# Three quarters of the second feed-forward product as Strassen's seven products, in place of eight

## The chip, the cores and the metric

The kernel runs on one core of one Trainium2 chip. The metric is the device time of one execution in microseconds; the median of the timed runs is compared. TensorE (PE) multiplies, VectorE (DVE) and ScalarE (ACT) work element by element, GpSimd (POOL) does a little arithmetic, and the DMA queues of SyncE (SP) and ACT bring the weights in. In the profile "PEld" is the loading of the stationary operand into TensorE.

## The reference, cut to what matters

Two blocks run one after the other over 512 tokens of 1024 features. The first has two layers, each a mixture of a dilated attention and an mLSTM and then a feed-forward part; the second has two mixers (an MLA and a gated linear attention), each steered by scale, shift and gate rows that come from a condition vector (`modulation`). The change is in the feed-forward part of the first block:

```python
D_MODEL = 1024
SEQ = 512
D_FF = 4 * D_MODEL
...
    h2 = rms_norm(x, norm_mlp_w)
    x = x + jnp.square(jax.nn.relu(h2 @ w_ff1)) @ w_ff2
    return x
```

All of it is float32. `w_ff1` is 1024 x 4096 and `w_ff2` is 4096 x 1024 in each of the two layers.

## The kernel before, in words

**Exact products.** Every large product is made of three matmuls in the type float32r: each operand is split into a high and a low part (`Prog.split`: ACT writes the high part, L246, and DVE subtracts it from the source, L247), and `mm3` (L274 to L277) multiplies high by high, high by low and low by high into one PSUM bank. A matmul holds a 128 x 128 stationary tile and streams 512 columns (256 in one place).

**The feed-forward part** (`first_block`, L666 to L704) goes in steps b of 512 of the 4096 hidden features. A *feature step* takes one unit of `w_ff1` (128 x 1024 numbers, loaded by the SP queue into `raw`, split into `spl`), issues 24 matmuls into a bank of the pool A, and evacuates it: ACT takes the relu (L678), DVE squares it (L679), and ACT and DVE split the square into the two parts of `big`. In the first step of a layer each of the four units is used in two half steps of 256 tokens. Four feature steps give 512 hidden features of all 512 tokens. `add_wide` (L732) then multiplies them with four units of `w_ff2`: eight groups of 12 matmuls, each evacuated by DVE into the residual stream `x` (L737). The last 512 features are added token tile by token tile, so that the next stage's norm can begin.

**Beside it: the modulation rows** (`Modulation`, L787 to L827). `start` loads the conditions (`cond`, on the ACT queue), takes a tanh on ACT (L803) and a product on DVE (L804) and issues the first two loads of `ada` on the ACT queue. Each of 24 calls of `use` per layer then reduces one 128 x 1024 unit of `ada` with three DVE instructions (L817 twice, L819 once) and issues a load two units ahead (L810). Its tiles come from the pools that the whole first block shares, so its instructions may be placed as soon as the attention's tiles are free.

**What sets the order.** A scheduler turns the program into one list of instructions for each engine, and each engine works its list strictly from the front. An instruction that must wait holds up everything behind it on its engine; a DMA issue on the ACT list is such an instruction too. Tiles come from pools with a fixed number of places; a new tile waits until the last reader of the old one in its place is done. In the feed-forward part the pool A has two banks, `spl` four places and `raw` two.

## Time and profile before

| quantity | value |
|---|---|
| median of 3 runs (lowest to highest) | 2380.8 us (2378.7 to 2384.31) |
| span of the profiled execution | 2376.0 us |
| PE busy | 2336.0 us, 98% of the span, 12280 matmuls |
| DVE busy | 1438.8 us, 61% |
| ACT busy | 961.2 us, 40% |
| POOL busy | 48.5 us, 2% |
| chain that ended last | PE 84%, DVE 8%, ACT 3%, DMA 2%, issue 2% |

The profiled execution's own time is its span; the median of the timed runs is 4.8 us above it, and all working below is made against the span. Matmuls are pipelined, so the busy time of one (377 ns in the mean for the largest group) is not the distance from one to the next; that distance is read from a stretch that PE fills. The page's granted clock of TensorE reads 9 (full speed) in each of its 40 slices.

### The profile page before, as it was taken

Reading aid. Unit: us, or ns where it says so; the run is one execution under the profiler, and the core shown is the slowest. Engines: PE = TensorE matmul, PEld = TensorE weight load, DVE = VectorE, ACT = ScalarE, POOL = GpSimd, SP = SyncE. Lnnn points to the kernel's source line nnn. Section 1 sums busy time; section 2 is a strip of 40 time slices with the busy share of each in tenths; the row PEclk is TensorE's granted clock in tenths of the full one; section 3 lists DMA queues with packets and bytes.
Section 4 is the critical chain, followed back from the end, with each engine's and each line's share of the span. In section 5 each row is a group of like instructions: output and inputs, shape, how many; then the busy total and the mean of one; then the engine's idle time right before and its main releaser. Section 6 shows DMA issues by size and latency. Waiting matters only on the chain.

```text
span 2376.0 us, 30969 instructions
## 1 busy us (share of the span) xinstructions
PE 2336.0 (98%) x12280; PEld 1904.2 (80%) x12280; DVE 1438.8 (61%) x2534; ACT 961.2 (40%) x1809; POOL 48.5 (2%) x96
## 2 busy tenths in 40 slices
PE   8999999999999999999999999999999999999998
PEld 6777888888888777788888888789888888788886
DVE  4477795544444547779654444454477776647486
ACT  3356422422322226642342232333366783363332
POOL 0000000000000000000000000010000000000000
PEclk9999999999999999999999999999999999999999
DMA  4221463222323222146432222312110130121111
GB/s 152 80 82 48 166 215 124 92 94 89 106 89 99 83 80 72 54 152 215 136 106 98 89 98 98 97 39 89 45 28 19 24 88 22 59 88 36 48 51 71
DMA packets 61345, 209.24 MB, mean 88 GB/s; under 512 B 8576, under 2 KB 9872, under 8 KB 60944
## 3 DMA queue, kind: packets, MB, share of 16 engines
q1 hardware_dynamic: 54000, 179.99, 23.4%
q10 hardware_dynamic: 7200, 27.27, 3.5%
q8 instruction: 97, 1.59, 0.3%
q14 instruction: 48, 0.39, 0.1%
HBM read 201.99 MB, written 2.10 MB: 86 GB/s over the span
## 4 chain that ended last, share of the span: by engine, by line
PE 84%; DVE 8%; ACT 3%; DMA 2%; issue 2%; POOL 1%; SPq 0%; ACTq 0%; POOLq 0%; DVEq 0%
PE A L277 22%; PE A L276 22%; PE A L275 21%; PE O L1133 2%; PE T L1125 2%; DVE spl L247 2%; PE S L275 1%; PE O L512 1%; PE S L276 1%; PE S L277 1%; PE S L486 1%; DMA ada<-in_ada 1%; PE T L506 1%; DVE junk L817 1%; ACT spl L246 1%
## 5 line engine op out<-in xcount | busy, mean ns | idle before, releaser
L246 ACT ACTIVATE spl<-raw 128x1024 fp32r<-128x1024 f32 (+2 forms) x313 | 325.0, 1040 | 477.0 <-PE A L277 429.6
L275 PE MATMUL A<-big,spl 128*128 128x512 f32 (+1 forms) x1280 | 483.0, 377 | 1.9 <-DVE x L737 1.2
L277 PE MATMUL A<-big,spl 128*128 128x512 f32 (+1 forms) x1280 | 481.4, 376 | 0.2 <-DVE spl L247 0.2
L276 PE MATMUL A<-big,spl 128*128 128x512 f32 (+1 forms) x1280 | 480.8, 376 | 0.0
L247 DVE TENSOR_TENSOR spl<-raw,spl 128x1024 fp32r<-128x1024 f32 (+2 forms) x313 | 375.8, 1204 | 163.1 <-ACT spl L246 161.7
L276 PE MATMUL A<-spl,big 128*128 128x512 f32 (+2 forms) x992 | 384.7, 389 | 1.1 <-DVE spl L247 1.0
L275 PE MATMUL A<-spl,big 128*128 128x512 f32 (+2 forms) x992 | 383.6, 388 | 1.6 <-ACT big L246 0.8
L277 PE MATMUL A<-spl,big 128*128 128x512 f32 (+2 forms) x992 | 381.8, 385 | 0.2 <-DVE ms L284 0.2
L277 PEld LDWEIGHTS A<-big,spl 128*128 128x128 f32 x1280 | 241.1, 188 | 45.9 <-issue 2.6
L275 PEld LDWEIGHTS A<-big,spl 128*128 128x128 f32 x1280 | 241.2, 188 | 45.1 <-DVE x L737 1.6
L276 PEld LDWEIGHTS A<-big,spl 128*128 128x128 f32 x1280 | 241.2, 188 | 43.3 <-issue 1.4
L275 PEld LDWEIGHTS A<-spl,big 128*128 128x128 f32 x992 | 186.3, 188 | 44.2 <-ACT big L246 2.8
L276 PEld LDWEIGHTS A<-spl,big 128*128 128x128 f32 x992 | 186.7, 188 | 40.3 <-DVE spl L247 3.0
L277 PEld LDWEIGHTS A<-spl,big 128*128 128x128 f32 x992 | 186.6, 188 | 39.2 <-issue 1.5
L737 DVE SCALAR_TENSOR_TENSOR x<-A,x 128x512 f32<-128x512 f32 x160 | 110.0, 688 | 121.7 <-PE A L277 119.9
L679 DVE TENSOR_TENSOR r<-r 128x512 f32<-128x512 f32 (+1 forms) x72 | 45.5, 633 | 170.9 <-ACT r L678 170.9
L678 ACT ACTIVATE r<-A 128x512 f32<-128x512 f32 (+1 forms) x72 | 39.7, 551 | 219.8 <-PE A L277 219.6
L1100 DVE TENSOR_REDUCE mx<-S 128x1 f32<-128x768 f32 (+1 forms) x80 | 71.8, 900 | 26.7 <-PE S L277 25.8
L1126 ACT ACTIVATE pt<-T 128x512 f32<-128x512 f32 (+1 forms) x144 | 66.5, 501 | 32.2 <-PE T L1125 31.1
L286 POOL TENSOR_TENSOR rstd<-ms,mhalf 128x1 f32<-128x1 f32 (+2 forms) x68 | 42.4, 623 | 1765.1 <-DVE ms L284 1720.8
L1105 ACT ACTIVATE p<-S,mx 128x768 f32<-128x768 f32 (+1 forms) x96 | 72.6, 760 | 13.8 <-DVE mx L1100 12.9
L817 DVE SCALAR_TENSOR_TENSOR junk<-ada,cond 128x512 f32<-128x512 f32 x96 | 65.7, 687 | 6.1 <-DMA ada<-in_ada 4.9
(413 smaller groups left out, 3438.8 us busy)
## 6 DMA issues: line engine op xcount, KB each, us to landing
raw<-in_wl SPq DMA_DIRECT2D x244, 512.0 KB, 3.2
ada<-in_ada ACTq DMA_DIRECT2D x48, 512.0 KB, 3.8
raw<-in_gla SPq DMA_DIRECT2D x33, 512.0 KB, 3.2
raw<-in_mla SPq DMA_DIRECT2D x20, 512.0 KB, 3.3
raw<-in_mla SPq DMA_DIRECT2D x8, 384.0 KB, 2.9
qT<-rot SPq DMA_DIRECT2D x32, 96.0 KB, 2.8
x<-in_x SPq DMA_DIRECT2D x4, 512.0 KB, 10.2
big<-in_wl SPq DMA_DIRECT2D x4, 512.0 KB, 9.3
```

Of the source, the lines that this page charges most:

```text
L246: nc.scalar.activation(hi, src, AF.Copy)
L247: nc.vector.tensor_tensor(lo, src, f32(hi), op=OP.subtract)
L275: mm(ps, lh, rh, start=start, stop=False)
L276: mm(ps, lh, rl, start=False, stop=False)
L277: mm(ps, ll, rh, start=False, stop=stop)
L737: P.nc.vector.scalar_tensor_tensor(xv, ps, scale, xv, op0=OP.mult, op1=OP.add)
L817: nc.vector.scalar_tensor_tensor(junk, w[:, o], 0.5, self.cond[:, 0, o], op0=OP.mult, op1=OP.mult, accum_out=self.acc[:, g, j:j + 1])
L1100: nc.vector.tensor_reduce(mx[:, 0:two], pss[:, 0:two * m].rearrange("p (t n) -> p t n", t=two), AX.X, OP.max, negate=True)
L1105: nc.scalar.activation(p[:, t * m:(t + 1) * m], pss[:, t * m:(t + 1) * m], AF.Exp, bias=mx[:, t:t + 1], accum_out=sl[:, t:t + 1])
L1125: nc.tensor.transpose(pst[:, k:k + 128], p[:, o + k:o + k + 128], P.ident)
L1126: nc.scalar.activation(pt[:, o:o + w], pst[:, 0:w], AF.Copy)
L1133: nc.tensor.matmul(weigh.o[64 * i:64 * i + 64, (t0 + t) * 128:(t0 + t + 1) * 128], V[4 * c + k][:, h * 64:(h + 1) * 64], pts[i][:, t * m + ...
```

## The change

The first 3072 of the 4096 hidden features are taken in three chunks of 1024. For a chunk the second product is a 2 x 2 block product: token halves (256) by feature halves (512) times feature halves by column halves (512). The class `Seven` computes it with seven block products (24 matmuls each) of sums of quarters, in place of eight; the remaining 1024 features go through `add_wide` as before. A chunk's seven products stand in turn with the eight feature steps of the next chunk.

- The squares stay whole (float32) in `big` or `hidden`; sums of their quarters (`total`, on DVE, L867) or the quarters themselves are split for each product (`part`).
- The quarters of `w_ff2` are loaded as tiles of 128 x 2048 (`quarter`); sums of them are made in place on POOL (`gather`, L863, two halves of 128 x 1024 each), and two units are split for each product. There are four gathers, eight POOL instructions, in a chunk.
- The products accumulate in two pairs of banks, X and Y, that stay allocated; after a product DVE adds the bank, with a sign, into `x` (L850), and a later product goes on accumulating on what stands there.
- The pools of the attention and the mLSTM are closed before the feed-forward part, and its own pools are opened in their place. `mod.start` takes its tiles from these new pools, and `use` takes its `junk` from the pool `relu`, of two places, which also holds the relu's output.
- Comments and blank lines differ throughout (left out here), and the DMA scratch is set to 1024.

```diff
+QUARTERS = ((0, 0), (0, 1), (1, 1), (1, 0))
...
     f1, f2 = a["w_ff1"][l], a["w_ff2"][l]
-    for b in range(9):
-        if b < 8:
-            u += [_tall(f1, 512 * b + 128 * j) for j in range(4)]
-        if b:
-            for ch in range(2):
-                u += [_wide(f2, 4 * (b - 1) + k, 512 * ch) for k in (0, 2)]
+    u += [_tall(f1, 128 * j) for j in range(32)]
+    for b in (6, 7):
+        for ch in range(2):
+            u += [_wide(f2, 4 * b + k, 512 * ch) for k in (0, 2)]
     return np.stack(u)
+
+def pack_quarters(a, l):
+    w = a["w_ff2"][l][0:3072].reshape(3, 2, 4, 128, 2, 512).transpose(0, 1, 4, 3, 2, 5)
+    return np.stack([w[:, i, j] for i, j in QUARTERS], axis=1).reshape(12, 128, 2048)
...
     for l in range(2):
+        mixing = ExitStack()
+        rest = P.pool("big", 1, mixing, side="right")
+        vp, tmp, one, pp = (P.pool(n, k, mixing) for n, k in (("vp", 1), ("tmp", 2), ("one", 1), ("pp", 3)))
...
+        mixing.close()
         act2 = act_of(norm.dst)
+        after = ExitStack()
+        vp, tmp, one = (P.pool(n, k, after) for n, k in (("vp2", 1), ("tmp2", 3), ("one2", 1)))
         mod.start(l, vp)
-        fs = {}
-        for b in range(9):
-            if b < 8:
-                fs[b] = big((3, 4, 2)[b % 3])
-                ws = [W() for _ in range(4)] if b == 0 else None
-                for n0, n1 in ((0, 256), (256, 512)) if b == 0 else ((0, 512),):
+        seven = Seven(P, xs, A[f"wq{l}"], P.pool("parts", 3, after), P.pool("quarter", 4, after), tmp)
+        hid, rr = P.pool("hidden", 1, after), P.pool("relu", 2, after)
+        def features(c):
+            f = fs[c] = big(2, F32) if c % 2 == 0 else hid.tile([128, 2, 4, 512], F32, name="hidden")
+            for i in range(2):
+                ws = [W() for _ in range(4)] if c + i == 0 else None
+                for n0, n1 in ((0, 256), (256, 512)) if c + i == 0 else ((0, 512),):
                     for j in range(4):
                         ps = P.bankA()
                         tall(ps, ws[j] if ws else W(), act2, range(8), n0, n1)
-                        r = tmp.tile([128, 512], F32, name="r", tag="yf")[:, n0:n1]
+                        r = rr.tile([128, 512], F32, name="r")[:, n0:n1]
                         nc.scalar.activation(r, ps[:, n0:n1], AF.Relu)
-                        nc.vector.tensor_tensor(r, r, r, op=OP.mult)
-                        P.split(fs[b][:, 0, j, n0:n1], fs[b][:, 1, j, n0:n1], r)
-            for g in range(24 * b // 9, 24 * (b + 1) // 9):
-                mod.use(l, g, tmp, "u")
+                        nc.vector.tensor_tensor(f[:, i, j, n0:n1], r, r, op=OP.mult)
+                        yield
+        fs, chunks = {}, iter(range(24))
+        for c in range(4):
+            more = seven.chunk(c - 1, fs[c - 1]) if c else iter(())
+            for i, _ in enumerate(features(c)):
+                if i % 4 < 3:
+                    for g in itertools.islice(chunks, 1):
+                        mod.use(l, g, rr, "r")
+                next(more, None)
+            for _ in more:
+                pass
...
+        last = [[seven.part(seven.of(fs[3], i, j), seven.quarter, "quarter") for i in range(2)] for j in range(2)]
...
+            add_wide(P, W, lambda t, k: seven.cut(last[j][t // 2], t % 2, k), xs, 1.0, done)
...
+class Seven:
+    def __init__(self, P, xs, units, parts, quarter, tmp):
+        self.P, self.xs, self.units, self.parts, self.quarter, self.tmp = P, xs, units, parts, quarter, tmp
+        self.X, self.Y = [P.bankS(), P.bankS()], [P.bankS(), P.bankO()]
...
+    def part(self, src, pool=None, tag="part"):
+        u = (pool or self.parts).tile([128, 2, 4, 256], F32R, name="part", tag=tag)
+        self.P.split(u[:, 0], u[:, 1], src)
+        return u
...
+    def product(self, ps, a, b, start, to):
+        P, nc = self.P, self.P.nc
+        u, ws = self.part(a), []
+        for i in range(2):
+            w = P.spl.tile([128, 2, 1024], F32R, name="spl")
+            P.split(w[:, 0], w[:, 1], b[:, i * 1024:(i + 1) * 1024])
+            ws.append(w.rearrange("p s (k n) -> p s k n", k=2))
+        for t in range(2):
+            for k in range(4):
+                w = ws[k // 2]
+                P.mm3(ps[t], *self.cut(u, t, k), w[:, 0, k % 2], w[:, 1, k % 2], start and k == 0, k == 3, skip_group_check=not start)
+            r, c, sign = to
+            x = self.xs[2 * r + t][:, 512 * c:512 * c + 512]
+            nc.vector.scalar_tensor_tensor(x, ps[t], sign, x, op0=OP.mult, op1=OP.add)
+    def chunk(self, c, f):
...
+        def gather(d, x):
+            for i in range(2):
+                v = d[:, i * 1024:(i + 1) * 1024]
+                nc.gpsimd.tensor_tensor(v, v, x[:, i * 1024:(i + 1) * 1024], op=OP.add)
...
+        self.product(self.X, a11, b11, True, (0, 0, 1.0))
+        gather(b11, b12)
+        d = total(a21, a22, OP.subtract)
+        self.product(self.Y, d, b11, True, (1, 1, 1.0))
+        gather(b11, b22)
+        s = total(d, a11, OP.subtract)
+        self.product(self.X, s, b11, False, (0, 1, -1.0))
+        s = total(a12, s, OP.add)
+        self.product(self.Y, s, b22, False, (0, 1, 1.0))
+        gather(b12, b22)
+        self.product(self.X, total(a11, a21, OP.subtract), b12, False, (1, 1, -1.0))
+        gather(b11, b21)
+        self.product(self.Y, a12, b21, True, (0, 0, 1.0))
+        self.product(self.X, a22, b11, False, (1, 0, 1.0))
...
-    nc = bacc.Bacc("TRN2", target_bir_lowering=False, num_devices=1)
+    nc = bacc.Bacc("TRN2", target_bir_lowering=False, num_devices=1, dynamic_dma_scratch_size=1024)
```

ACT at the opening of the feed-forward part of the first layer, before: `r` is the relu of a half step, `big` the norm's output (from the transposes T) and then the high part of a square.

```order
L246 ACTIVATE big_3253<-T_3461 128x4x128 [waits PE_49]
L246 ACTIVATE big_3254<-T_3468 128x4x128 [waits PE_49]
L678 ACTIVATE r_3529<-A_3504 128x256 [waits PE_49]
L246 ACTIVATE big_3483<-r_3529 128x256 [waits DVE_49]
L678 ACTIVATE r_3559<-A_3534 128x256 [waits PE_49]
L246 ACTIVATE big_3483<-r_3559 128x256 [waits DVE_49]
L678 ACTIVATE r_3589<-A_3564 128x256 [waits PE_49,Activation_49]
L246 ACTIVATE big_3483<-r_3589 128x256 [waits DVE_49]
```

The same place in the changed kernel: L909 loads the conditions, L911 is the tanh, L918 the load of a unit of `ada`, L695 the relu.

```order
L252 ACTIVATE big_3253<-T_3461 128x4x128 [waits PE_49]
L252 ACTIVATE big_3254<-T_3468 128x4x128 [waits PE_49]
L909 DMA cond_3489<-in_cvec 128x2048
L695 ACTIVATE r_3559<-A_3534 128x256 [waits PE_49]
L911 ACTIVATE ada_3491<-cond_3489 128x2048 [waits DMAHW6_49]
L918 DMA ada_3491<-in_ada0 128x1024 [waits DVE_49]
L918 DMA ada_3491<-in_ada0 128x1024 [waits DMAHW5_49]
L695 ACTIVATE r_3592<-A_3567 128x256 [waits PE_49]
L695 ACTIVATE r_3625<-A_3600 128x256 [waits DVE_49,PE_49]
L918 DMA ada_3491<-in_ada0 128x1024 [waits DMAHW7_49,DVE_49]
L918 DMA ada_3491<-in_ada0 128x1024 [waits DMAHW0_49,DVE_49]
L695 ACTIVATE r_3658<-A_3633 128x256 [waits PE_49,Activation_49]
```

The whole chain of `mod.start` has moved from the projections before the feed-forward part to its opening, in front of the second, third and fourth relu.

DVE in the middle of the feed-forward part, before: the end of a group of feature steps, and the start of its `add_wide`.

```order
L679 TENSOR_TENSOR r_4143<-r_4143 128x512 [waits Activation_49]
L247 TENSOR_TENSOR spl_4266<-raw_4264,spl_4266 128x1024 [waits DMAHW2_49,PE_49,Activation_49]
L247 TENSOR_TENSOR big_4042<-r_4143,big_4042 128x512 [waits Activation_49]
L679 TENSOR_TENSOR r_4178<-r_4178 128x512 [waits Activation_49]
L247 TENSOR_TENSOR spl_4271<-raw_4269,spl_4271 128x1024 [waits DMAHW3_49,PE_49,Activation_49]
L247 TENSOR_TENSOR big_4042<-r_4178,big_4042 128x512 [waits Activation_49]
L737 SCALAR_TENSOR_TENSOR x0_74<-A_4208,x0_74 128x512 [waits PE_49]
L737 SCALAR_TENSOR_TENSOR x1_75<-A_4222,x1_75 128x512 [waits PE_49]
```

DVE in the changed kernel from the square of the last feature step of a chunk (the second chunk of the first layer): L696 squares, L867 makes a `total`, L253 is the low part of a split, L925 and L927 are a `use`, L850 adds a product to `x`.

```order
L696 TENSOR_TENSOR hidden_3935<-r_4496 128x512 [waits Activation_49]
L867 TENSOR_TENSOR total_4621<-hidden_3935 128x1024 [waits DVE_49]
L253 TENSOR_TENSOR spl_4584<-raw_4582,spl_4584 128x1024 [waits DMAHW4_49,PE_49,Activation_49]
L867 TENSOR_TENSOR total_4698<-total_4621,hidden_3935 128x1024 [waits DVE_49]
L253 TENSOR_TENSOR part_4623<-total_4621,part_4623 128x1024 [waits Activation_49]
L925 SCALAR_TENSOR_TENSOR junk_4533,acc_3494<-ada_3491,cond_3489 128x512 [waits DMAHW2_49]
L696 TENSOR_TENSOR big_4499<-r_4530 128x512 [waits Activation_49]
L925 SCALAR_TENSOR_TENSOR junk_4533,acc_3494<-ada_3491,cond_3489 128x512 [waits DVE_49]
L253 TENSOR_TENSOR spl_4626<-quarter_4538,spl_4626 128x1024 [waits PE_49,Activation_49]
L927 SCALAR_TENSOR_TENSOR ada_3491,acc_3494<-ada_3491,cond_3489 128x1024 [waits DVE_49]
L850 SCALAR_TENSOR_TENSOR x0_74<-S_3503,x0_74 128x512 [waits PE_49]
L253 TENSOR_TENSOR part_4700<-total_4698,part_4700 128x1024
```

Where the list held splits, squares and evacuations, it now holds the totals and the splits of `part` and the calls of `use` among them, in one line.

## Rows read from the trace of the kernel before

**Rows 1.** The page: busy time and share of each engine.

```profile
PE 2336.0 (98%) x12280; PEld 1904.2 (80%) x12280; DVE 1438.8 (61%) x2534; ACT 961.2 (40%) x1809; POOL 48.5 (2%) x96
```

**Rows 2.** Busy time by stretches: projections, steady feed-forward; columns as in the first line.

```profile
core 0: us, PE busy (x) PEld busy (x) DVE busy (x) ACT busy (x) POOL busy (x), PEclk, DMA share, GB/s
...
470.00:776.00 306.00, 306.00 (x1336) 250.38 (x1335) 139.37 (x168) 86.65 (x111) 0.50 (x1) 1.00 0.29 96
300.00:400.00 100.00, 99.92 (x437) 81.45 (x436) 81.25 (x154) 27.91 (x34) 0.33 (x3) 1.00 0.54 179
```

**Rows 3.** Groups by line and shape, first layer's feed-forward part (440 to 800 us).

```profile
L678 ACT ACTIVATE r<-A 128x512 f32<-128x512 f32 x28 | 16.8, 600 | 101.5 <-PE A L277 101.5
...
L678 ACT ACTIVATE r<-A 128x256 f32<-128x256 f32 x7 | 2.7, 384 | 8.6 <-PE A L277 8.6
```

**Rows 4.** Timeline of PE in a half step: start us, us, instruction.

```profile
439.03 0.28 PE L275 MATMUL A<-big,spl 128*128 128x256 f32 x1
439.15 0.28 PE L276 MATMUL A<-big,spl 128*128 128x256 f32 x1
```

**Rows 5.** Timelines of ACT and DVE where the modulation starts, first layer.

```profile
254.29 0.38 ACTq L801 DMA_DIRECT2D cond<-in_cvec  x1
...
261.00 1.91 ACT L803 ACTIVATE ada<-cond 128x2048 f32<-128x2048 f32 x1
...
265.26 0.82 ACTq L810 DMA_DIRECT2D ada<-in_ada  x2
...
262.94 2.29 DVE L804 SCALAR_TENSOR_TENSOR cond<-ada,cond 128x2048 f32<-128x2048 f32 x1
```

**Rows 6.** DMA issues: KB each, median us from issue to landing.

```profile
ada<-in_ada ACTq DMA_DIRECT2D x48, 512.0 KB, 3.8
...
cond<-in_cvec ACTq DMA_DIRECT2D x2, 1024.0 KB, 5.1
```

**Rows 7.** Timeline of DVE where its instructions follow without a wait.

```profile
312.43 0.68 DVE L817 SCALAR_TENSOR_TENSOR junk<-ada,cond 128x512 f32<-128x512 f32 x1
...
313.15 0.69 DVE L817 SCALAR_TENSOR_TENSOR junk<-ada,cond 128x512 f32<-128x512 f32 x1
...
313.89 1.23 DVE L819 SCALAR_TENSOR_TENSOR ada<-ada,cond 128x1024 f32<-128x1024 f32 x1
...
318.22 1.22 DVE L247 TENSOR_TENSOR spl<-raw,spl 128x1024 fp32r<-128x1024 f32 x1
319.36 0.68 DVE L658 SCALAR_TENSOR_TENSOR tg<-tg,A 128x512 f32<-128x512 f32 x1
319.96 0.68 DVE L817 SCALAR_TENSOR_TENSOR junk<-ada,cond 128x512 f32<-128x512 f32 x1
```

**Rows 8.** POOL and DVE at once: two casts, timeline and durations (min/median/max).

```profile
1702.07 3.87 POOL L1023 CAST kT<-kT 32x1536 fp32r<-32x1536 f32 x2 [68.07 <-DVE kT L247]
...
1702.15 2.45 DVE L247 TENSOR_TENSOR spl<-raw,spl 128x1024 fp32r<-128x1024 f32 x1 [0.22 <-ACT spl L246]
1704.64 1.03 DVE L247 TENSOR_TENSOR kT<-T,kT 32x256 fp32r<-32x256 f32 x2
...
L1023 POOL CAST kT<-kT x2: 1457/1959/2461, 1702.1 to 1703.5; 32x1536 fp32r<-32x1536 f32 x2
```

**Rows 9.** POOL's small operation beside DVE, timelines of two moments.

```profile
1580.03 0.95 DVE L247 TENSOR_TENSOR spl<-raw,spl 128x768 fp32r<-128x768 f32 x1
...
1580.26 1.13 POOL L286 TENSOR_TENSOR rstd<-ms,mhalf 128x1 f32<-128x1 f32 x1 [2.12 <-DVE ms L284]
...
1566.60 0.55 POOL L286 TENSOR_TENSOR rstd<-ms,mhalf 128x1 f32<-128x1 f32 x1 [3.43 <-DVE ms L284]
...
1566.37 0.68 DVE L737 SCALAR_TENSOR_TENSOR x<-A,x 128x512 f32<-128x512 f32 x1
```

**Rows 10.** Busy time by stretches at PE's longest pauses; columns as in rows 2.

```profile
2365.00:2370.00 5.00, 2.59 (x12) 1.81 (x10) 3.83 (x5) 0.86 (x1) 0.52 (x1) 1.00 0.26 105
2370.00:2376.00 6.00, 0.00 (x0) 0.00 (x0) 1.44 (x2) 0.29 (x2) 0.55 (x1) 0.67 0.21 87
...
2150.00:2155.00 5.00, 3.00 (x15) 2.30 (x15) 4.70 (x9) 1.71 (x4) 0.00 (x0) 1.00 0.00 0
```

## The prediction

> **What bounds the kernel now.** I read the page's busy line first: PE works 98% of the span, DVE 61%, POOL almost nothing [rows 1]. An average can hide stages, so the windows came next. Over 306 us of steady feed-forward PE has no gap, 1336 matmuls stand in it, and DVE works 139 us of it [rows 2]. So this stage is bound by PE, DVE is at 46%, and a matmul is worth 306 / 1336 = 0.229 us, not the longer busy time of a single one, which overlaps its neighbours. Then I read ACT, DVE and POOL instruction by instruction, because the change gives them the work that PE loses, in lists that each engine follows strictly. The sum below is made against the profiled span, 2376.0 us; the median of the timed runs, 2380.8, is 4.8 above it, and I add that at the end.

> **Term A, the matmuls removed.** A chunk had eight block products of 24 matmuls and has seven. Three chunks in each of two layers: 6 x 24 = 144 matmuls, 144 x 0.229 = 33.0 us saved. It is whole if DVE and ACT keep ahead of PE, and two places say that they will not.

> **Term B, the opening of the feed-forward part.** The chain of `mod.start` used to run in the projections. Its tiles now lie where the attention's were, so it opens the feed-forward part, and ACT's list has it in front of the second, third and fourth relu. There ACT waits for a DMA, then for DVE. I count from the end of PE's first half step; a half step is 24 matmuls of 256 columns at 0.12 [rows 4] = 2.88 us. The condition load takes 5.1 from issue to landing [rows 6], the tanh 1.9, DVE's product 2.3: 9.3 us. Two DMA issues on ACT (0.8) [rows 5] and the relu (0.38 [rows 3]) bring the second relu to 10.5. PE meanwhile fills the pool's two banks with half steps 2 and 3, 5.8 us, and then waits: 4.7 us. The `ada` units issued at about 9.4 land 3.8 later [rows 6], at 13.2; DVE's first reduction (0.7 [rows 7]), a square (0.4) and a relu (0.4) bring the third relu to 14.8, where PE could have gone on at 13.4: 1.4 us. The next pair of issues stands behind the reductions that free both `ada` places, about 5 us of DVE: 19.4, plus an issue and a relu 20.1, against 17.7: 2.4 us. Sum 8.5 us a layer, 17 for both. The bounds are 0, if the loads start before the part begins and all of it is covered, and 10.5, if no half step covers any; 8.5 is what the rows' own durations give.

> **Term C, DVE in the middle of a chunk.** The tightest stretch of DVE's list runs from the square of a chunk's last feature step to the second split of the fourth product's quarter. It holds 13 splits and 4 totals of 1024 columns at a pitch of 1.14, 4 squares and 5 evacuations at 0.60 and three calls of `use` at 0.72 + 0.74 + 1.23 = 2.69 [rows 7]: 19.4 + 5.4 + 8.1 = 32.9 us. It starts 0.9 after PE ends the feature step: 0.60 for the relu [rows 3] and 0.3 that I allow for the last matmul's tail (0.28 against a pitch of 0.12 [rows 4]) and the hand-over. So DVE is ready at 33.8. PE arrives after seven steps of 24 matmuls and 6 more: 174 x 0.229 = 39.8. There are 6.0 us to spare if DVE is never held up.

> It will be held up, I think, by POOL. Each chunk has eight halves of a gather, additions of 128 x 1024 with both inputs in SBUF, an operation that the trace of before never shows at this size. What it does show is a cast of 1536 columns on POOL: 1.46 us alone; when it met a DVE split, the split took 2.45 for its usual 1.22 and ended where the first cast would, and the other cast took 2.46, until the next split was over [rows 8]. So one of the two waits while the other runs. A small POOL operation took 1.13 beside a split and 0.55 beside an evacuation from PSUM [rows 9]; evacuations are not held.

> [...]

> The price of a half: at the cast's rate with one input, 1.46 x 1024 / 1536 = 0.97; two inputs read in turn at that rate 1.94; that plus the 0.55 of a tiny POOL operation 2.49; the whole cast's time twice 2.9. These are the bounds, 0.97 to 2.9; I take 2.2, the middle of the two readings that count two inputs. A `gather` also runs in place, in front of the next product's splits, but its wait lies inside the same hold.

> In chunks 2 and 3 POOL starts early: three halves fall while DVE waits for PE, five in the stretch: 11.0, less three evacuations beside them (1.8), 9.2. That is 9.2 - 6.0 = 3.2 us of PE idle in each. In chunk 1 DVE comes out of the opening with nine calls of `use` behind it and no pause, so all eight fall in the stretch: 17.6, less four evacuations (2.4) and 1.0 that I allow for moments in which DVE waits for ACT anyway: 14.2, 8.2 us late. A layer loses 8.2 + 3.2 + 3.2 = 14.6, both 29.2.

> **What I cost at nothing.** ACT has its share of the extra splits, but works 87 of 306 us in this stage [rows 2]. SP loads the same bytes (DMA 29% busy there), and a chunk's quarters are issued a chunk ahead; if late they would show as POOL waiting for a DMA. `use` leaves the projections, but PE was at 99.92% there [rows 2], so nothing comes back; it is DVE time in the stage where DVE is now short. The evacuation of products into `x` stands in DVE's list ahead of splits, waiting for PE; it is in the tally above. The end of a layer still goes through `add_wide`, its first parts are made beside the last products. A chunk's DVE work, 67 to 73 us by the same pitches, lies under the 360 x 0.229 = 82.4 of its matmuls, but with 17.6 us of holds it would nearly fill it: no reserve catches up what the middle loses.

> **Sum.** -33.0 + 17.0 + 29.2 = +13.2; span 2389.2, time 2394.

> **The rivals.**
> - *The holds are cheap.* At 0.97 a half, or if POOL always finds a gap, the middle costs nothing (5 x 0.97 - 1.8 = 3.1, under the 6.0; chunk 1: 8 x 0.97 - 3.4 = 4.4), and the opening alone is paid: -33.0 + 17.0, time 2365, faster. For it: DVE is at 46% before. Against it: the cast and the split excluded each other in both directions, and two inputs should not cost POOL what one does. Chance 0.20.
> - *The opening is covered, the holds are not.* If the scheduler's placing lets the condition load start well before PE's first half step: -33.0 + 29.2, time 2377. Against it: the load has a place in ACT's list behind the norm's last split, whose wait ends just before. Chance 0.12.
> - *Neither*, the whole gain: 2348. Chance 0.12.
> - *The holds are at the far end*, 2.9 a half: chunks 2 and 3 lose 14.5 - 7.8 = 6.7, chunk 1 23.2 - 9.4 = 13.8, a layer 8.5 + 27.2 = 35.7; time 2419. [...] Chance of either 0.14.

> **How the numbers follow.** The forecast has 0.42. Its own range takes the hold between 1.94 and 2.49: 36.8 or 56.6 us of idle in all, so 2385 to 2404. To hold eight cases in ten I go down to the edge of the second and first rivals, 2356, leaving out the whole gain (0.12), and up to 2413, leaving out about half of the last rival. A measurement of this kernel tells about 0.2% from no change, 2376 to 2386. Faster: 0.20 + 0.12 + about half of the second rival + 0.01 = 0.39. Same: the other half of it and the low end of the forecast, 0.14. Slower: the rest, 0.47.

> **What would show it.** PE's matmuls must fall by 144. At the opening of each layer's feed-forward part PE should show three waits for ACT's relu, near 4.7, 1.4 and 2.4 us, and ACT a wait for the DMA of `cond`. In each chunk PE should wait for DVE's splits in products 2 to 4, more in the first chunk than later. DVE splits beside a gather should last 2 to 3.4 us, the gather's halves about 2.2 alone, and evacuations 0.68 as ever. The clock row should stay at 9. If PE is at 99% in the chunks, the holds were overrated and the time is near 2365; if the half steps follow without a gap, term B is wrong; if PE waits for `quarter` or `part` through DMA or ACT, the reason is another one than mine.

## The result

The changed kernel takes 2407.0 us (median of 4 runs, 2404.3 to 2409.3), the kernel before beside it 2380.5: a ratio of 1.011, 95% interval 1.0096 to 1.0124. It is slower, as forecast, but by 26.5 us where 13.2 were worked out. The span of the profiled execution is 2407.5 us, 31.5 above that of before.

The page's busy line of the changed kernel, to be read beside [rows 1]:

```profile
PE 2328.0 (97%) x12136; PEld 1889.3 (78%) x12136; DVE 1585.6 (66%) x2560; ACT 1010.6 (42%) x1823; POOL 192.0 (8%) x144
```

144 matmuls are gone (12280 before), and PE is busy only 8.0 us less, not 33. So the lost time shows in two forms: PE stood still longer (span less busy: 79.5 us, before 40.0), and its matmuls took longer. What PE waited for in the changed kernel, by total (engine, bank and line; releaser; us, times, longest):

```profile
PE S L282 <- DVE spl L253: 22.0, 13, 2.8
PE A L281 <- ACT r L695: 15.6, 5, 7.8
PE T L755 <- DVE xn L301: 8.8, 1, 8.8
```

The third is the start of the kernel, as before (10.1). The first two are new: the middle of the chunks and the opening of the feed-forward parts.

**The opening, first layer.** ACT's timeline (start, us, instruction, idle time before it and what ended it); [rows 5, 6] are what it was worked out from:

```profile
438.61 0.38 ACTq L909 DMA_DIRECT2D cond<-in_cvec  x1
...
439.91 0.39 ACT L695 ACTIVATE r<-A 128x256 f32<-128x256 f32 x1
447.19 1.91 ACT L911 ACTIVATE ada<-cond 128x2048 f32<-128x2048 f32 x1 [6.90 <-DMA cond<-in_cvec]
451.46 0.82 ACTq L918 DMA_DIRECT2D ada<-in_ada  x2
452.33 0.38 ACT L695 ACTIVATE r<-A 128x256 f32<-128x256 f32 x1 [3.22 <-DVE cond L912]
460.53 0.38 ACT L695 ACTIVATE r<-A 128x256 f32<-128x256 f32 x1 [7.82 <-DVE junk L925]
462.23 2.43 ACTq L918 DMA_DIRECT2D ada<-in_ada  x2
464.75 0.38 ACT L695 ACTIVATE r<-A 128x256 f32<-128x256 f32 x1 [3.84 <-DVE ada L927]
```

The chain is the one that was forecast, step by step, but its DMAs are slow: `cond` lands 8.6 us after its issue (438.61 to 447.2), `ada` about 7.3 (451.46 to 458.8), for 5.1 and 3.8. The windows over the same stretch show why, and what came of it; columns as in [rows 2], the clock is the third number from the end, then DMA share and GB/s:

```profile
440.00:445.00 5.00, 4.92 (x42) 4.72 (x40) 2.32 (x4) 0.29 (x2) 0.00 (x0) 1.00 0.87 297
445.00:450.00 5.00, 0.00 (x0) 0.00 (x0) 0.86 (x1) 1.91 (x1) 0.00 (x0) 0.68 1.01 415
450.00:455.00 5.00, 2.24 (x10) 2.24 (x11) 1.43 (x1) 0.38 (x1) 0.00 (x0) 0.50 1.03 402
455.00:460.00 5.00, 2.77 (x16) 2.56 (x14) 1.21 (x4) 0.00 (x0) 0.00 (x0) 0.80 0.60 241
460.00:465.00 5.00, 4.04 (x23) 4.04 (x24) 4.29 (x11) 0.63 (x2) 0.00 (x0) 0.66 0.32 105
465.00:470.00 5.00, 5.00 (x44) 4.96 (x43) 4.46 (x11) 3.71 (x6) 0.00 (x0) 1.00 0.43 123
```

The DMA engines are full, with a share of 1.01 and 1.03 from 445 to 455 us: the four quarters of the first chunk, 1 MB each, are loaded just then (issued from 433.1 to 443.2, landing 10.3 to 13.0 us later). PE stands still for 7.8 us, and the clock goes from 1.00 to 0.50; the matmuls that follow start every 0.21 us in place of 0.12. The clock is back at 1.00 before the next pause, 3.2 us (457.77 to 460.96), and falls again 0.5 us before its end: 0.50 from 460.5 to 463.9.

**The middle of a chunk, second chunk of layer 1.** First DVE, then POOL, in the same microseconds:

```profile
589.08 3.30 DVE L867 TENSOR_TENSOR total<-hidden 128x1024 f32<-128x1024 f32 x1
592.30 3.42 DVE L253 TENSOR_TENSOR spl<-raw,spl 128x1024 fp32r<-128x1024 f32 x1
595.65 1.21 DVE L867 TENSOR_TENSOR total<-total,hidden 128x1024 f32<-128x1024 f32 x1
...
602.02 0.68 DVE L850 SCALAR_TENSOR_TENSOR x<-S,x 128x512 f32<-128x512 f32 x1
602.62 2.82 DVE L253 TENSOR_TENSOR part<-total,part 128x1024 fp32r<-128x1024 f32 x1
605.37 0.68 DVE L850 SCALAR_TENSOR_TENSOR x<-S,x 128x512 f32<-128x512 f32 x1
605.97 1.21 DVE L253 TENSOR_TENSOR spl<-quarter,spl 128x1024 fp32r<-128x1024 f32 x1
```

```profile
582.76 11.89 POOL L863 TENSOR_TENSOR quarter<-quarter 128x1024 f32<-128x1024 f32 x4 [46.67 <-DVE spl L253]
601.03 3.33 POOL L863 TENSOR_TENSOR quarter<-quarter 128x1024 f32<-128x1024 f32 x1 [6.39 <-DVE spl L253]
```

The same shape takes DVE 1.21 us when POOL is idle, and 2.8 to 3.4 when a half of a gather runs; the evacuation at 602.02, in the middle of a half, takes its 0.68. POOL pays too: over the kernel a half takes 2372 ns at least, and 3270 in the median. The split at 605.97 is what PE waits for, in 1 us windows (columns as above):

```profile
605.00:606.00 1.00, 0.29 (x2) 0.00 (x0) 1.00 (x3) 0.00 (x0) 0.00 (x0) 1.00 0.01 4
606.00:607.00 1.00, 0.00 (x0) 0.00 (x0) 1.00 (x2) 0.00 (x0) 0.00 (x0) 1.00 0.00 0
607.00:608.00 1.00, 0.77 (x2) 0.67 (x3) 1.00 (x2) 0.00 (x0) 0.74 (x1) 0.61 0.00 0
608.00:609.00 1.00, 1.00 (x4) 0.81 (x3) 1.00 (x2) 0.00 (x0) 1.00 (x1) 0.50 0.00 0
609.00:610.00 1.00, 1.00 (x4) 0.71 (x4) 1.00 (x1) 0.00 (x0) 1.00 (x1) 0.50 0.79 131
610.00:611.00 1.00, 1.00 (x5) 0.82 (x4) 1.00 (x1) 0.00 (x0) 0.55 (x1) 0.68 0.87 348
```

PE pauses for 1.95 us, and the clock then stands at 0.50 for 3.4 (607.23 to 610.64). Whether that is a second price of the same wait, e12 tells.

### The profile page after: what moved, and what is told of

Same layout as the page of the kernel before. It is cut to its first block, busy times and chain, and to the rows that moved or that the text cites. A ratio compares the mean times of both kernels' runs of the same rounds, so it can differ in the third digit from the quotient of the medians.

```text
span 2407.5 us, 30741 instructions
## 1 busy us (share of the span) xinstructions
PE 2328.0 (97%) x12136; PEld 1889.3 (78%) x12136; DVE 1585.6 (66%) x2560; ACT 1010.6 (42%) x1823; POOL 192.0 (8%) x144
## 4 chain that ended last, share of the span: by engine, by line
PE 73%; DVE 16%; issue 4%; ACT 4%; DMA 4%; POOL 0%; SPq 0%; ACTq 0%; POOLq 0%; DVEq 0%
PE A L283 16%; PE A L282 16%; PE A L281 16%; DVE spl L253 5%; PE S L281 3%; PE S L282 2%; PE S L283 2%; PE O L1241 2%; PE T L1233 2%; DVE junk L925 2%; DVE part L253 2%; DMA ada<-in_ada 1%; DVE ada L927 1%; PE O L522 1%; DVE total L867 1%
## 5 line engine op out<-in xcount | busy, mean ns | idle before, releaser
L281 PE MATMUL A<-big,spl 128*128 128x512 f32 (+1 forms) x1280 | 486.0, 380 | 17.5 <-ACT r L695 15.6
L253 DVE TENSOR_TENSOR spl<-raw,spl 128x1024 fp32r<-128x1024 f32 (+2 forms) x265 | 334.3, 1264 | 206.2 <-ACT spl L252 204.6
L252 ACT ACTIVATE spl<-raw 128x1024 fp32r<-128x1024 f32 (+2 forms) x265 | 274.5, 1037 | 360.6 <-PE A L283 260.5
L281 PE MATMUL A<-spl,big 128*128 128x512 f32 (+2 forms) x480 | 181.7, 382 | 1.8 <-ACT spl L252 1.0
L282 PE MATMUL A<-spl,big 128*128 128x512 f32 (+2 forms) x480 | 181.7, 380 | 1.8 <-DVE spl L253 1.8
L283 PE MATMUL A<-spl,big 128*128 128x512 f32 (+2 forms) x480 | 181.8, 379 | 0.2 <-DVE ms L290 0.2
L863 POOL TENSOR_TENSOR quarter<-quarter 128x1024 f32<-128x1024 f32 x48 | 143.3, 2988 | 399.1 <-DVE spl L253 398.2
L253 DVE TENSOR_TENSOR spl<-quarter,spl 128x1024 fp32r<-128x1024 f32 x84 | 121.1, 1442 | 13.1 <-ACT spl L252 13.1
L282 PE MATMUL S<-spl,part 128*128 128x512 f32 x264 | 107.8, 408 | 22.5 <-DVE spl L253 22.0
L252 ACT ACTIVATE spl<-quarter 128x1024 fp32r<-128x1024 f32 x84 | 87.3, 1054 | 64.5 <-PE S L283 29.7
L281 PEld LDWEIGHTS A<-spl,big 128*128 128x128 f32 x480 | 90.2, 189 | 20.3 <-ACT spl L252 3.2
L283 PE MATMUL S<-spl,part 128*128 128x512 f32 x264 | 105.9, 401 | 0.0
L282 PEld LDWEIGHTS A<-spl,big 128*128 128x128 f32 x480 | 90.6, 189 | 19.5 <-DVE spl L253 3.6
L281 PE MATMUL S<-spl,part 128*128 128x512 f32 x264 | 105.1, 398 | 0.0
L283 PEld LDWEIGHTS A<-spl,big 128*128 128x128 f32 x480 | 90.5, 189 | 16.8 <-issue 1.3
L695 ACT ACTIVATE r<-A 128x512 f32<-128x512 f32 (+1 forms) x72 | 39.2, 544 | 146.8 <-PE A L283 92.9
```

The lines of the kernel that those rows point to most:

```text
L252: nc.scalar.activation(hi, src, AF.Copy)
L253: nc.vector.tensor_tensor(lo, src, f32(hi), op=OP.subtract)
L281: mm(ps, lh, rh, start=start, stop=False, **more)
L282: mm(ps, lh, rl, start=False, stop=False, **more)
L283: mm(ps, ll, rh, start=False, stop=stop, **more)
L695: nc.scalar.activation(r, ps[:, n0:n1], AF.Relu)
```

## The experiments

The kernel before, run beside all of them, took 2379.6 to 2381.4 us in the median. "Idle" is the span less PE's busy time.

| run | median us | span | PE busy | idle |
|---|---|---|---|---|
| before | 2380.5 | 2376.0 | 2336.0 | 40.0 |
| changed | 2407.0 | 2407.5 | 2328.0 | 79.5 |
| e1 gathers on DVE | 2368.3 | 2366.4 | 2312.4 | 54.0 |
| e2 no gathers | 2365.5 | 2367.4 | 2312.8 | 54.6 |
| e3 early modulation | 2397.6 | 2396.9 | 2326.7 | 70.2 |
| e4 e1 and e3 | 2358.7 | 2357.9 | 2309.9 | 48.0 |
| e5 e1, shared pool | 2347.9 | 2345.9 | 2304.1 | 41.8 |
| e9 e5, late reductions | 2345.0 | 2342.6 | 2303.3 | 39.3 |
| e6 eight products | 2407.6 | 2402.8 | 2348.7 | 54.1 |
| e7 useless matmuls | 2420.9 | 2419.1 | 2340.9 | 78.2 |
| e10 holds only | 2424.7 | 2422.7 | 2333.3 | 89.4 |
| e11 half on POOL | 2377.4 | 2377.4 | 2316.0 | 61.4 |
| e12 e9, gathers on POOL | 2388.9 | 2387.5 | 2317.9 | 69.6 |

**e1, gathers on DVE.**

```diff
-                nc.gpsimd.tensor_tensor(v, v, x[:, i * 1024:(i + 1) * 1024], op=OP.add)
+                nc.vector.tensor_tensor(v, v, x[:, i * 1024:(i + 1) * 1024], op=OP.add)
```

> The gathers (sums of quarters of w_ff2) run on DVE in place of POOL; nothing else changes. Theory A (POOL's gathers hold DVE's two-input instructions for 2.4 to 3.3 us each, DVE becomes late, PE pauses, and pauses over 2 us also halve the clock for some us): the middle of the chunks loses about 42 us in the changed kernel; on DVE a half costs about 1.14, 9.1 us a chunk, under what the holds take, so about 34 of the 42 come back: about 2373 us (2365 to 2385), DVE splits at 1.22 us again, PE's waits for DVE's splits under 6 us in all. Theory B (DVE simply has too much of its own work in the chunks, POOL is incidental): DVE gets 55 us more, so slower than the changed kernel, 2415 us or more.

Measured 2368.3, faster than before (ratio 0.9952, 0.9939 to 0.9964). DVE got 57 us more of its own work and lost the holds; its groups (count, busy us, mean ns):

```profile
L253 DVE TENSOR_TENSOR spl<-quarter,spl 128x1024 fp32r<-128x1024 f32 x84 | 101.7, 1218 | 11.4 <-ACT spl L252 10.9
L863 DVE TENSOR_TENSOR quarter<-quarter 128x1024 f32<-128x1024 f32 x48 | 57.1, 1216 | 0.1
```

In the changed kernel the mean of the first was 1442. Theory B falls: more work on DVE made the kernel 39 us faster.

**e2, no gathers.** `gather` does nothing, so the sums of `w_ff2` are left out.

> The gathers are left out: each product multiplies with the single quarter as loaded (so w_ff2's sums are missing from the result). Matmuls, splits, totals and loads are those of the changed kernel. Theory A: all of the middle's loss goes, 2407 - 42 = about 2365 us, and PE waits for splits no longer in products 2 to 4; only the opening's pauses stay. Theory B: DVE's list is as full as before, so PE still waits for splits, and the time stays above 2395 us.

Measured 2365.5. PE's waits, the largest:

```profile
PE A L281 <- ACT r L695: 14.2, 4, 6.6
PE T L755 <- DVE xn L301: 10.6, 1, 10.6
PE L L1485 <- DVE acc L1468: 2.0, 1, 2.0
PE A L282 <- DVE spl L253: 1.5, 4, 0.5
```

The waits of products for splits are gone, and 41.5 us with them; only the opening is left. Moving the gathers to DVE (e1) gets all but 3 us of that.

**e3, early modulation.** A pool `modp` that lives through the block takes the place of `vp` in `mod.start`.

```diff
     ck = P.pool("ck1", 1, st)
+    mp = P.pool("modp", 1, st)
...
-        mod.start(l, vp)
+        mod.start(l, mp)
```

> The condition, its tanh and product and the first two loads of ada get tiles of their own that live through the whole block, so that they no longer stand at the opening of the feed-forward part; the gathers stay on POOL. Theory A: the opening's loss goes (14.7 us in layer 1, some 6 in layer 2 with the clock), a few us may be paid at the start of the kernel: about 2388 us (2382 to 2395), granted clock 1.00 in the opening. Rival C (the opening pauses come from the crowded DMA queues: four quarters of 1 MB are loaded at that moment): PE then waits for raw units instead, and at most 8 us come back: 2399 us or more.

Measured 2397.6: 9.4 us back, where 19 were expected; between theory and rival. Two things are left. The fourth relu still stands behind two `ada` issues that wait for DVE, a pause of about 3 us in each layer (PE for ACT's relu: 6.2 us, 2 times). And the loads went to the start of the kernel, where everything up to the feed-forward part came 5 us later (the norm's transposes at 439.0 for 434.0). PE waits for no `raw` unit in this opening, so it is not the crowded queues alone that stop it; e5 shows what the chain's place in the list is worth.

**e4, both.**

> Both edits: gathers on DVE and the early start of the modulation. Theory A: the two losses are independent, 2407 - 34 - 19 = about 2354 us (2348 to 2365), faster than the kernel before by about 1%. If they share a cause (DVE in arrears from the opening), the sum of the two gains is more than half missing: above 2375 us.

Measured 2358.7, ratio 0.9911 (0.9897 to 0.9924). Against e1 the early start brings 9.6, against the changed kernel 9.4: the two losses add up.

**e5, shared pool.** In place of `modp`, the pool `vp` lives through the block, with the attention's tiles in the same places, as in the kernel before (gathers on DVE).

> Gathers on DVE, and the modulation's condition and ada tiles lie in one pool shared with the attention's, as in the kernel before, so that its start may run in the projections. Theory A: as e4 (2359) but without the about 4 us that e4 pays at the start of the kernel: about 2355 us (2351 to 2359); a pause of about 3 us a layer stays at the fourth half step, where ACT issues two ada loads that wait for the first two reductions. If the opening's cost were the tiles' late space and not the wait in ACT's list, nothing would differ from e1: 2368 us.

Measured 2347.9, 7 us better than expected: the 4 us at the start of the kernel came back, and in layer 2 the pause at the fourth half step did not appear at all. From e1 that is 20 us for the place of one chain in ACT's list, with as much DMA and DVE work as there.

**e9, late reductions.**

```diff
-                if i % 4 < 3:
+                if (i > 2 if c == 0 else i % 4 < 3):
```

> As e5, and the nine reductions of the first chunk begin after the fourth half step, not the first (the same nine, without the gaps). Theory A: the last pause of the opening (3 us and the slow clock behind it, some 4 us a layer) goes: about 2347 us (2343 to 2352), which is the kernel before less the 33 us of its removed matmuls, PE without a pause over 1 us in both feed-forward parts. If the reductions then press DVE in the first chunk instead, PE waits for splits there and the gain is under 3 us.

Measured 2345.0, ratio 0.9851 (0.9837 to 0.9864): the fastest version. Its span is 33.4 us under that of before, where the removed matmuls were put at 33.0. The stretch where e5 still pauses, e5 first, then e9 (windows, columns as above):

```profile
450.00:455.00 5.00, 3.57 (x30) 3.36 (x29) 0.88 (x3) 0.00 (x0) 0.00 (x0) 1.00 0.90 368
455.00:460.00 5.00, 3.42 (x18) 3.43 (x19) 4.96 (x13) 3.61 (x5) 0.00 (x0) 0.72 0.32 109
460.00:465.00 5.00, 5.00 (x37) 4.82 (x36) 5.00 (x12) 1.83 (x3) 0.00 (x0) 0.93 0.77 247
```

```profile
450.00:455.00 5.00, 5.00 (x44) 5.00 (x43) 5.00 (x10) 2.66 (x4) 0.00 (x0) 1.00 0.65 256
455.00:460.00 5.00, 5.00 (x40) 4.87 (x40) 4.69 (x11) 1.83 (x3) 0.00 (x0) 1.00 0.87 262
```

Without the pause the clock stays at 1.00.

**e6, eight products.** `chunk` without sums: each of the eight block products by `product`, in turn into X and Y, with sign 1.

> The changed kernel's tiles, pools, order and openings, but eight plain products of quarters in a chunk: no sums on DVE, no gathers, 144 matmuls more. Theory A: the no-gather run (2365.5) plus 144 x 0.229 = 33: about 2398 us (2394 to 2402), so the new structure alone costs some 20 us, all of it at the openings. If the sums of the squares (seven totals a chunk on DVE) also cost PE time in the changed kernel, it comes out lower: 2390 us or less.

Measured 2407.6, above the expected range; against e2 it is 42 us by the medians and 35.4 by the profiled spans, where 33 was put. The opening of layer 1 is as in e1 (pauses of 6.2 and 2.8 us). In that of layer 2 the scheduler has put transposes of the second block's norm into PE's list, and PE waits there for their operands, 1.3 and 5.0 us, in place of the relus (3.8 and 1.0 in e1):

```profile
PE T L936 <- DVE xn L301: 5.3, 2, 5.0
```

So in this arrangement seven products with POOL's gathers gain nothing over eight without: the gathers eat what the eighth product gave. There is no sign that the sums on DVE cost PE time.

**e7, useless matmuls in the pause.** Eight matmuls of 128x512 into a bank of T in the second product, before the second split is needed.

> The changed kernel with eight matmuls of no use (128x512, into a free bank) put into the second product of each chunk, ahead of the split that PE waits for there 2.3 to 3.2 us: 48 matmuls more that fall into PE's pauses. Theory A1 (the slow clock after a pause is a loss of its own): the pauses shrink under 1.5 us, the clock stays at 1.00 there, six times about 1.6 us come back: about 2397 us although PE has more work. Theory A2 (DVE's arrears set the end of the chunk's middle; what the clock takes from PE is time that PE would wait for DVE at the next product): PE waits longer at the third and fourth products, the time stays within 3 us of the changed kernel's 2407.

Measured 2420.9: neither. The scheduler counts the new matmuls and changed DVE's list: in the third product `part` of the next product now stands ahead of the second split that PE waits for, one split (and its hold) later. The pause moved there (PE waits for splits: 4 in each layer, up to 3.0 us), and behind the first of 3.0 us the matmuls start every 0.43 us in place of 0.23, as they do in the changed kernel at a clock of 0.50. So the run itself does not tell how much of the slow clock could have been saved; e12 does.

**e10, holds only.** Products take quarters as loaded where the changed kernel takes gathered ones; the 48 additions on POOL stay.

```diff
-        self.product(self.Y, d, b11, True, (1, 1, 1.0))
+        self.product(self.Y, d, b12, True, (1, 1, 1.0))
```

(and b22 for b11, b22 for b12, b21 for b11 in the third, fifth and last product)

> The changed kernel with its 48 gather halves on POOL as before, but no product uses a gathered quarter where a plain one can stand: the products multiply with quarters as loaded (so w_ff2's sums are missing from the result), and no split waits for POOL except by the shared tiles. Theory H (POOL's two-input additions hold DVE's two-input instructions; that alone makes DVE late): the loss stays, 2395 us or more, splits beside a gather at 2.5 to 3.4 us. Rival L (the loss is the latency of the chain split, gather, split through POOL, 2.4 to 3.3 us a link where DVE takes 1.2): near the run without gathers, 2366 us.

Measured 2424.7. With nothing to wait for from POOL but the shared tiles, the additions cost more than before; in the later chunks six of them now run back to back (18.59 us), before at most four. POOL, then DVE, at the start of the first chunk:

```profile
491.44 8.02 POOL L863 TENSOR_TENSOR quarter<-quarter 128x1024 f32<-128x1024 f32 x3 [54.26 <-DMA ada<-in_ada]
```

```profile
491.60 2.80 DVE L925 SCALAR_TENSOR_TENSOR junk<-ada,cond 128x512 f32<-128x512 f32 x1 [0.23 <-DMA ada<-in_ada]
...
494.32 2.88 DVE L696 TENSOR_TENSOR big<-r 128x512 f32<-128x512 f32 x1
497.12 2.89 DVE L925 SCALAR_TENSOR_TENSOR junk<-ada,cond 128x512 f32<-128x512 f32 x1
```

Three instructions of 0.68 us each take 2.8 to 2.9: own time and one half of a gather, 2.2 us, in turn. Rival L falls; the hold alone makes DVE late.

**e11, half on POOL.**

```diff
+                (nc.vector if i else nc.gpsimd).tensor_tensor(v, v, x[:, i * 1024:(i + 1) * 1024], op=OP.add)
```

> Of each gather the first half stays on POOL and the second goes to DVE (24 halves on each). Theory H: per chunk 4 holds of about 2.2 and 4 additions of 1.14 on DVE are 13.4 us in place of 17.6, so 4.2 a chunk and 25 us in all come back, less where DVE already had a margin: about 2382 us (2376 to 2392), between e1 (2368) and the changed kernel (2407). Rival L (latency of the chain): the first half still passes POOL in each gather, so little comes back: 2398 us or more.

Measured 2377.4: 30 us back by half the dose. The waits for splits shrink from 22.0 us to this, none over 1.3:

```profile
PE S L282 <- DVE spl L253: 4.9, 6, 1.3
```

That is a margin being crossed, not a price per gather. From the square of a chunk's last feature step to the second split of its fourth product, the second chunk's DVE list is held twice, 3.2 us in all, where the changed kernel has seven held instructions and 12.0 us; what is left DVE can nearly spare. In the middle of both layers the granted clock stays at 1.00.

**e12, the best version with the gathers back on POOL.** The edit of e1 undone in e9.

> The best version so far (2345: gathers on DVE, the modulation's start in the projections, late reductions) with the gathers put back on POOL: the changed kernel without its opening's pauses. Theory: the two losses are independent, so the gathers cost their 40 us here too: about 2385 us (2380 to 2390), no faster than the kernel before. If DVE's arrears from the opening were part of the gathers' cost, the gathers cost less than 30 here: under 2375 us.

Measured 2388.9, ratio 1.0032 (1.0019 to 1.0045). PE's first wait:

```profile
PE S L282 <- DVE spl L253: 29.9, 16, 4.4
```

The gathers cost 44.9 us of span here and 41.1 with the opening's pauses in place; the losses are independent to within 4 us.

This run also shows what the slow clock behind a pause is worth. The second chunk of layer 1, from the first matmul of its first product to the last of its seventh, in the changed kernel and then in e12 (each time the first 26 us, then all of it):

```profile
592.40:618.40 26.00, 24.05 (x98) 19.22 (x97) 26.00 (x28) 9.76 (x11) 11.46 (x4) 0.93 0.21 64
592.40:669.00 76.60, 74.45 (x312) 59.33 (x311) 70.15 (x86) 30.73 (x34) 14.60 (x5) 0.98 0.41 141
```

```profile
581.50:607.50 26.00, 24.09 (x104) 19.07 (x102) 26.00 (x28) 10.03 (x12) 11.45 (x4) 1.00 0.20 66
581.50:658.10 76.60, 72.96 (x312) 58.08 (x311) 70.15 (x86) 30.73 (x34) 14.59 (x5) 1.00 0.41 142
```

Both pause about 1.9 us in the second product. Behind it the clock falls in the changed kernel and stays at 1.00 in e12, and the 312 matmuls end in the same 76.6 us. DVE works the same list in both, each start within 0.04 us, with no gap in the first 26: it sets when PE may go on. With the faster clock PE only waits again, 1.7 us in the third product. The slow matmuls took the place of a wait, and cost nothing here.

## Why the prediction was right, and where its sizes came from

Three differences of the table split the change's 31.5 us of span without a rest. Before to e9: seven products for eight, with nothing in the way. E9 to e1: the opening. E1 to the changed kernel: the gathers on POOL.

| term | forecast | span | PE busy | idle |
|---|---|---|---|---|
| A, matmuls removed | -33.0 | -33.4 | -32.7 | -0.7 |
| B, opening | +17.0 | +23.8 | +9.1 | +14.7 |
| C, DVE held in the middle | +29.2 | +41.1 | +15.6 | +25.5 |
| sum | +13.2 | +31.5 | -8.0 | +39.5 |

- **Term A** held: 144 x 0.229 by the pitch of a stretch that PE fills. The busy time of a single matmul would have given 54.
- **Term B**: mechanism and place were right; the size was not. In layer 1 the fourth relu ends 25.2 us after the first begins (439.91 to 465.13), where 20.1 was worked out. The two DMAs had been taken at their landing times from a quiet stretch, 5.1 and 3.8 [rows 6]; beside 4 MB of quarters they took 8.6 and 7.3. In layer 2, whose quarters were issued 26 us and more before the condition load, that load lands after 5.0, and the same count is 18.6. PE waits 7.8 and 3.2 us in layer 1 and 3.3 and 1.0 in layer 2, where 4.7, 1.4 and 2.4 stood for each. That the idle sum came out near (14.7 for 17.0) is luck: slow matmuls fill part of the longer wait.
- **Term C**: a half was priced at 2.2 us between 0.97 and 2.9; it takes 2.37 when nothing stops it and holds a DVE instruction up to 2.1 or 2.2 (3.30 for 1.21, 2.80 for 0.68). Splits, totals, squares and the reductions of `use` were held: splits up to 3.44 for 1.22, totals 3.43 for 1.21, squares 2.87 and reductions 2.70 for 0.68. The exemption of evacuations held: the 84 into `x` (L850) take 0.67 to 0.69. One reading of [rows 8] was off: the held split ended 1.07 us after the first cast, not with it (1704.60 and 1703.53); that one waits for the other stays.
- **Where term C was too small.** From the first matmul of a chunk's first product to the last of its seventh, e1 takes 71.9 us in layer 1 and 71.6 in layer 2. The changed kernel takes 80.1, 76.6 and 76.9, and 79.5, 76.5 and 81.7: 8.2, 4.7, 5.0 and 7.9, 4.9, 10.1 us lost, where 8.2, 3.2, 3.2 were forecast for each layer. The tightest point was named rightly: PE pauses at the second split of product 2 in all six chunks (13.5 us of the 22.0), but DVE's delay grows from there to that of product 4. In the second chunk of layer 1 that split is done 39.5 us after the chunk's first matmul; at e1's pace PE needs it at 34.6.
- **The step that fell short** is "three halves fall while DVE waits for PE, five in the stretch", put at 9.2 us of holds. In chunks 2 and 3 only two start before the stretch, and seven instructions in it are held, 12.0 us in all. The third chunk of layer 2 loses twice as much: 2.4 us of DVE work that the tally did not have, for the modulation's end and the next block's norm, stands ahead of the fourth product's split, and the slow clock behind that pause costs another 2.6. The first chunk's number came out by luck: 11.9 us of holds for 14.2, and more of DVE's own work.
- **The clock.** "The clock row should stay at 9" failed; the page's tenths show it in one slice at 8. The clock fell to 0.50 in or behind three pauses of the openings and six of the middle, for 3.4 to 10.2 us each time, and the same 12136 matmuls take 24.7 us more of PE's busy time in the changed kernel than in e9 (2328.0 and 2303.3). This is not a price of its own: where DVE's or ACT's list sets the pace, PE would otherwise have waited, as e12's chunk shows. At the opening PE works at 0.50 from 452.8 to 457.0 and still waits 3.2 us for the third relu, and its next slow half step ends as the fourth relu does. Only behind the pause in the fourth product of layer 2's last chunk, where no wait follows, does it cost time that can be seen: from that pause's end to the fifth product 12.3 us, 9.7 in e1.
- **The rivals.** Cheap holds fall by e1 and e10, a covered opening by the pause of 7.8 us, the whole gain by the result itself, the far end, 2.9 a half, by holds of at most 2.2.

The forecast's number, 2394, is 13 us below the measured 2407; the stated range, 2356 to 2413, holds it, 6 us under its upper end. The direction and both causes were right; both sizes were too small.

## What to carry to other kernels

Before arithmetic goes to a nearly idle POOL, look at what DVE does in those microseconds: where its instructions had two inputs in SBUF, both engines took turns here (a split of 1.22 us took up to 3.44), and doing the sums on DVE itself (1.2 us) cost less than the hold (2.2). The wait that came to stand in ACT's list ahead of PE's evacuations cost its whole chain, 25.2 us to the end of the fourth relu, with the DMAs as slow as the stretch it moved into made them (8.6 and 7.3 us for 5.1 and 3.8). Do not count a pause of PE twice, as idle time and as the slow matmuls behind it, before looking at what sets the end of the stretch: in the middle of these chunks it was DVE's list, and the slow matmuls only filled a wait (76.6 us with and without them). To size such a stretch, add up the list of the engine that sets the pace, with its holds, to the last instruction that PE needs.

## What the runs showed of the hardware that was not expected

```profile
2184.00:2185.00 1.00, 0.00 (x0) 0.00 (x0) 1.00 (x2) 0.00 (x0) 0.00 (x0) 1.00 0.00 0
2186.00:2187.00 1.00, 1.00 (x8) 1.00 (x7) 0.03 (x1) 0.00 (x0) 0.00 (x0) 1.00 0.00 0
```

```profile
2118.00:2119.00 1.00, 0.03 (x1) 0.06 (x1) 1.00 (x3) 0.00 (x0) 0.00 (x0) 1.00 0.00 0
2120.00:2121.00 1.00, 1.00 (x6) 1.00 (x6) 0.14 (x1) 0.00 (x0) 0.00 (x0) 0.50 0.00 0
```

- DVE and POOL took turns instruction by instruction: four halves in a row took 11.89 us (from 582.76), where four alone are 9.5. The halves ended at 585.16, 588.50, 591.30 and 594.64, and behind each of them one DVE instruction, at 586.24, 589.04, 592.38 and 595.72.
- Squares, whose two inputs are the same tile, were held like the others: 2.88 us for 0.68 in e10 (494.32), 2.87 in the changed kernel (495.58).
